# Gating a two-layer encoder's heads: where the product of heads and gates is made

## The chip, the cores and the metric

One core of one Trainium2 chip runs the whole program. Five engines work side by side and are tied together by semaphores only: TensorE (PE; its weight loads are shown apart as PEld), VectorE (DVE), ScalarE (ACT), GpSimd (POOL) and SyncE (SP), which here does nothing but issue transfers, in order. The metric is device microseconds per execution, the median of several runs. TensorE's clock has two levels, 2.4 and 1.2 GHz; the profile gives the granted share.

## What is computed

Two sequences (1024 and 512 tokens, width 1024) go through two layers and a final RMSNorm, all in float32. Layer 0 puts an attention of 8 heads (A) beside a retention of 4 heads (B); layer 1 is a windowed attention of 16 heads (C). In both, a gate of the same width as the heads is projected from the same input, goes through SiLU, and multiplies the heads before the one output projection:

```python
# layer 0
mixed = jnp.concatenate([jax.nn.silu(ga) * oa, jax.nn.silu(gb) * ob], axis=-1)
return x + mixed @ w_out
# layer 1
o = banded_sink_gqa(q, k, v, sink, rel_bias)
return x + (jax.nn.silu(gate) * o) @ w_out
# last
return rmsnorm(x, final_norm)
```

Only the place of the product `silu(gate) * o` is at stake here. Its values stay the same.

## The kernel before

**Tiling.** Tokens come in 12 blocks of 128, grouped into three groups t = 0, 1, 2 of 512 (0 and 1 are the long sequence, 2 the short one), and are worked on in the order 2, 0, 1. The width is split into 8 slices k of 128 rows, so that heads, gates and activations are 24 tiles [128, 512], one for each k and t. Every matmul runs on float32 operands split into a high and a low part (`X["h"]`, `X["l"]`, `split`), three products each. Layer 0's slices 0 and 1 hold the first four heads of A (g = 0), 2 and 3 the other four (g = 1), and 4 to 7 the heads of B. In layer 1, chunk c holds slices 2c and 2c+1.

**Attention.** `pipeline` (L722) goes through units of one head group and one 128-token block. For each unit `front_a` or `front_c` makes scores and softmax weights: VectorE takes maxima, ScalarE exponentiates, GpSimd scales the weights by the reciprocal sum (`scale_pool`, L107, tiles `e` and `ec`). `Back.T` transposes them, `Back.PV` multiplies by the values, and `Back.evac` (L700) brings the result `oT` [128, 2 x 128] from PSUM into SBUF. From there it is stored to DRAM (`o_ab` in layer 0, `o_c` in layer 1, L711). The buffers of tag O that hold `olo` and `oT` are two.

**Fillers.** While a unit passes through the other engines, TensorE gets filler steps of three matmuls: the gate projections (`gate_stream`, `gate_pieces`: 8 steps for each k and t, tile `psg`; then SiLU on VectorE, ScalarE and GpSimd, and a store of the finished gate to `g_ab` or `g_c`, L222), in layer 1 also the projections of the next queries (`psq`), and, once a group's attention is over, that group's output projection (`out_proj_fm`, tile `pso`).

**The mix.** When group t's attention is done, `hook_a` or `hook_c` calls `mix_fm` (L257): for each slice k it loads the heads and the gate back from DRAM into the two halves of one tile `mo`, multiplies them on GpSimd (L262) and splits the product into `X["h"]` (ScalarE, L117) and `X["l"]` (VectorE, L118) for the output projection. For some units the heads don't go to DRAM: `Back.mix` (L713) loads the unit's gates (`gq`, two transfers), multiplies on GpSimd (L719) and splits at once. That is so for g = 1 with t < 2 in layer 0 (8 units), and for c = 3 with t = 1 in layer 1 (4 units). Slices 2 and 3 of the last group never go through `mix_fm`.

**Order.** Each engine's queue is in order. A scheduler sets it from the order in which the code is written, from `tc.high_priority()` stretches and from its own view of the engines' times. A transfer that waits for its data or its buffer holds everything behind it on SP; likewise a product on GpSimd that waits for a gate holds the scalings behind it.

## Time and profile before

| | us |
|---|---|
| median of 3 runs | 1507.81 (1505.19 to 1508.24) |
| the profiled execution | 1507.83 |
| its span, first to last instruction | 1506.1 |
| TensorE busy | 1451.7 (96%) |
| VectorE busy | 1052.6 (70%) |
| GpSimd busy | 812.3 (54%) |
| ScalarE busy | 719.5 (48%) |

The program has stages: up to 300 us the input, keys and values and the retention; 310 to 590 us layer 0's attention with the gates as filler; 590 to 800 us the rest of that attention with the mix and the output projection; 800 to 920 us the last third of that projection and layer 1's keys; 920 to 1290 us layer 1's attention with gates and queries as filler; 1290 to 1460 us its end with the mix and the output projection; then the last third of the projection. A busy share over the whole span mixes these, so what counts is read by stage: which engines are nearly full there, where TensorE is idle, and which waits the chain goes through. Matmuls overlap, so a TensorE that reads as fully busy is not proven to be at its peak; the number of matmuls in a stretch (the x counts) says more.

### The profile page before, as it was taken

The page shows a single profiled execution, that of the slowest core. Times are in us where ns is not written, and L with a number is a line of the kernel's source. Part 1 is how long each engine was busy: PE and PEld are TensorE (multiplying, and loading weights), DVE is VectorE, ACT ScalarE, POOL GpSimd, SP SyncE. Part 2 cuts the span into 40 slices and gives each one's busy share as a digit, 9 for nine tenths or more (in the row PEclk, how much of TensorE's full clock was granted, in tenths as well). Part 3 has the DMA queues.
Part 4 walks back from the last instruction along what each step waited for, and adds up shares of the span by engine and source line. Part 5 has one row for each costly group of instructions (what it writes and reads, how often), then busy time and mean ns, then how long its engine had stood idle before and what let it go on. Part 6 is the DMA issues. An engine that isn't in the chain of part 4 may idle for free.

```text
span 1506.1 us, 26020 instructions
## 1 busy us (share of the span) xinstructions
PE 1451.7 (96%) x8734; PEld 1269.8 (84%) x8734; DVE 1052.6 (70%) x2431; ACT 719.5 (48%) x1770; POOL 812.3 (54%) x1044
## 2 busy tenths in 40 slices
PE   8999999989999999999999999999999999999997
PEld 8989999977888888777778998888888888777777
DVE  7455867686676666887978237687777767888774
ACT  5632222354555555555653245566556556645202
POOL 7654654474645484887887423342522532566542
PEclk9999999999999999999999999999999999999999
DMA  9631212326212143643664231121212211568752
GB/s 329 207 119 51 75 54 69 99 74 191 74 45 72 53 113 116 206 141 107 192 213 141 86 109 46 61 71 50 74 45 94 63 54 53 173 206 280 229 157 99
DMA packets 137333, 176.59 MB, mean 117 GB/s; under 512 B 38064, under 2 KB 66736, under 8 KB 137200
## 3 DMA queue, kind: packets, MB, share of 16 engines
q1 hardware_dynamic: 135040, 169.41, 35.8%
q0 software_dynamic: 2016, 5.51, 1.3%
q8 instruction: 69, 1.13, 0.3%
q14 instruction: 64, 0.52, 0.1%
q10 hardware_dynamic: 144, 0.01, 0.0%
HBM read 125.83 MB, written 53.25 MB: 119 GB/s over the span
## 4 chain that ended last, share of the span: by engine, by line
PE 71%; DVE 11%; DMA 4%; POOL 4%; issue 3%; ACT 1%; SPq 0%; POOLq 0%; DVEq 0%; ACTq 0%
PE psg L89 17%; PE psq L89 10%; PE po L89 8%; PE psb L89 8%; PE pso L89 8%; PE pte L173 7%; PE s L89 4%; PE sc L89 4%; PE pskv L89 2%; DVE xl L118 2%; DVE w L140 1%; DVE el L112 1%; DMA wraw<-in_woc 1%; DVE nm L837 1%; PE ptq L173 1%
## 5 line engine op out<-in xcount | busy, mean ns | idle before, releaser
L89 PE MATMUL psg<-xh,wg 128*128 128x512 f32 x768 | 263.9, 400 | 0.2 <-POOL wg L140 0.2
L107 POOL TENSOR_SCALAR ec<-ec,rl 128x384 f32<-128x384 f32 (+1 forms) x192 | 108.8, 581 | 241.5 <-DVE rl L1056 87.7
L112 DVE TENSOR_TENSOR el<-pte,eh 128x512 fp32r<-128x512 f32 x288 | 196.6, 685 | 56.2 <-ACT eh L111 32.5
L111 ACT ACTIVATE eh<-pte 128x512 fp32r<-128x512 f32 x288 | 170.1, 596 | 119.7 <-PE po L89 65.0
L89 PE MATMUL pso<-xh,w 128*128 128x512 f32 x512 | 183.6, 418 | 10.4 <-DVE w L140 4.6
L89 PEld LDWEIGHTS psg<-xh,wg 128*128 128x128 f32 x768 | 143.9, 189 | 29.2 <-POOL e L107 0.9
L107 POOL TENSOR_SCALAR e<-e,rl 128x512 f32<-128x512 f32 x160 | 114.3, 726 | 93.3 <-DVE rl L848 33.9
L89 PE MATMUL psg<-xl,wg 128*128 128x512 f32 x384 | 150.9, 393 | 0.0
L1051 ACT ACTIVATE ec<-ec,nm 128x384 f32<-128x384 f32 (+1 forms) x192 | 109.6, 572 | 82.7 <-DVE nm L1049 77.7
L845 ACT ACTIVATE e<-s,nm 128x512 f32<-128x512 f32 x160 | 108.9, 687 | 68.0 <-DVE nm L842 50.0
L837 DVE TENSOR_REDUCE nm<-s 128x1 f32<-128x512 f32 x160 | 107.8, 683 | 37.4 <-PE s L89 36.9
L139 POOL TENSOR_SCALAR w<-wraw 128x512 fp32r<-128x512 f32 x116 | 79.4, 686 | 97.6 <-PE pskv L89 32.4
L89 PE MATMUL psq<-xh,w 128*128 128x512 f32 x384 | 130.0, 397 | 0.0
L89 PEld LDWEIGHTS pso<-xh,w 128*128 128x128 f32 x512 | 99.4, 197 | 35.8 <-DVE w L140 7.8
L1045 DVE CUSTOM_DVE_ANT_0 ec<-sc,bias,sink_s 128x384 f32<-128x384 f32 (+1 forms) x192 | 105.3, 568 | 22.2 <-PE sc L89 17.8
L89 PE MATMUL pso<-xl,w 128*128 128x512 f32 x256 | 104.1, 408 | 2.0 <-DVE xl L118 2.0
L173 PE MATMUL pte<-ident,e 128*128 128x128 f32 x640 | 96.0, 275 | 1.6 <-POOL e L107 0.8
L173 PEld LDWEIGHTS pte<-ident,e 128*128 128x128 f32 x640 | 78.8, 142 | 20.3 <-ACT e L845 2.2
L140 POOL TENSOR_TENSOR w<-wraw,w 128x512 fp32r<-128x512 f32 x68 | 91.2, 1344 | 1.9
L89 PEld LDWEIGHTS psg<-xl,wg 128*128 128x128 f32 x384 | 72.5, 189 | 13.1
L89 PEld LDWEIGHTS psq<-xh,w 128*128 128x128 f32 x384 | 71.9, 188 | 13.6
L173 PE MATMUL pte<-ident,ec 128*128 128x128 f32 x512 | 79.0, 272 | 0.2
(230 smaller groups left out, 3942.6 us busy)
## 6 DMA issues: line engine op xcount, KB each, us to landing
wraw<-in_woab SPq DMA_DIRECT2D x48, 256.0 KB, 3.4
wraw<-in_woc SPq DMA_DIRECT2D x48, 256.0 KB, 3.8
wraw<-in_wab SPq DMA_DIRECT2D x44, 256.0 KB, 3.3
wraw<-in_wc SPq DMA_DIRECT2D x36, 256.0 KB, 3.1
xt<-in_xT SPq DMA_DIRECT2D x24, 256.0 KB, 5.4
xb<-in_x SPq DMA_DIRECT2D x24, 256.0 KB, 4.8
qd<-qd SPq DMA_DIRECT2D x48, 128.0 KB, 2.9
gab<-gz SPq DMA_DIRECT2D x24, 256.0 KB, 2.0
```

What stands on the lines that cost most here:

```text
L89: i = nc.tensor.matmul(ps, lhsT=lhsT, rhs=rhs, start=start, stop=stop)
L107: nc.gpsimd.tensor_scalar(o, i, s, 1.0, ALU.mult, ALU.mult)
L111: nc.scalar.activation(hi, src, AF.Copy)
L112: nc.vector.tensor_tensor(lo, src, hi.bitcast(F32), ALU.subtract)
L118: nc.vector.scalar_tensor_tensor(lo, src, scale, hi.bitcast(F32), ALU.mult, ALU.subtract)
L139: nc.gpsimd.tensor_scalar(w[:, 0, :], raw, 1.0, 1.0, ALU.mult, ALU.mult)
L140: (lo or nc.gpsimd).tensor_tensor(w[:, 1, :], raw, w[:, 0, :].bitcast(F32), ALU.subtract)
L173: return nc.tensor.transpose(o, i, ident)
L837: nc.vector.tensor_reduce(nm2[:, c:c + 1] if nh == 2 else nm[:, h:h + 1], s, AX.X, ALU.max, negate=True)
L845: nc.scalar.activation(eh[c], ss[c], AF.Exp, bias=nm[:, h:h + 1], accum_out=l[:, h, c:c + 1])
L1045: nc.vector.tensor_tensor_reduce(es[h][:, :nk], s, bias[h][:, bo:bo + nk], 1.0, sink_s[:, 4 * c + h:4 * c + h + 1], ALU.add, ALU.max, mx[: ...
L1051: nc.scalar.activation(es[a][:, :nk], es[a][:, :nk], AF.Exp, bias=nm[:, a:a + 1], accum_out=l[:, a:a + 1])
```

## The change

The product is made as soon as the later of heads and gate exists.

- **Layer 0, gates that come after their heads.** The gates of slices 4 to 7 are projected first, then 2 and 3, then 0 and 1. Where the heads of a gate are already stored, the finished gate is not stored: the heads are loaded (`go`, a buffer of tag `wraw`), and GpSimd multiplies the gate tile by them when the next piece has done its fourth step; only the product goes to `g_ab`. 18 of the 24 gates are of this kind (slices 0, 1, 4 to 7). `mix_fm` then loads one tile and multiplies nothing.
- **Layer 0, heads that come after their gates.** The 8 units of g = 1 and t < 2 load their gates when their second transpose is issued, and no longer at the evacuation, and the product is made as two products [128, 128] on VectorE instead of one [128, 256] on GpSimd. Slices 2 and 3 of t = 2 stay with two loads and a product in `mix_fm`.
- **Layer 1.** The gates are filled one set earlier (in the set before the first unit too), so that each unit finds its gates in DRAM. Every unit loads them early, two transfers of [128, 128], into unused columns of the bias tiles (which grow from 384 to 512 columns). 44 units multiply on GpSimd, two products [128, 128] between evacuation and store; the last 4 (c = 3, t = 1) multiply on VectorE. `mix_fm` loads one tile for each slice.

```diff
@@ -199,10 +199,20 @@
             hs.append(h)
         return hs
 
-    def gate_pieces(w, j, k, t, gd, scale):
+    stored, gated, owed = {}, set(), []
+
+    def settle():
+        while owed:
+            owed.pop(0)()
+
+    def gate_pieces(w, j, k, t, gd, od, scale):
+
+
         ps = ps_p("psg")
         for kk in range(KT):
             proj_fm_k(ps, w, j * P, t, kk)
+            if kk == 3:
+                settle()
             if kk < KT - 1:
                 yield
         with tc.high_priority():
@@ -219,15 +229,27 @@
             else:
                 nc.gpsimd.tensor_scalar(th, th, 1.0, 1.0, ALU.add, ALU.mult)
                 nc.gpsimd.tensor_tensor(z, th, z, ALU.mult)
+        if stored.get((id(od), k, t)) == GB:
+            o = wp.tile([P, 2 * CW], F32, tag="wraw", name="go", bufs=2)
+            dma(out=o, in_=od[k][t])
+            gated.add((id(gd), k, t))
+
+            def product():
+                nc.gpsimd.tensor_tensor(z, z, o, ALU.mult)
+                dma(out=gd[k][t], in_=z)
+            owed.append(product)
+        else:
             dma(out=gd[k][t], in_=z)
         yield
 
-    def gate_stream(warr, c0, gd, scale=None):
-        for c in range(4):
+    def gate_stream(warr, c0, gd, od, chunks, scale=None):
+        for c in chunks:
+            settle()
             w = load_w(warr, c0 + c, "wg")
             for t in ORDER:
                 for j in range(2):
-                    yield from gate_pieces(w, j, 2 * c + j, t, gd, scale)
+                    yield from gate_pieces(w, j, 2 * c + j, t, gd, od, scale)
+        settle()
 
     class Fill:
         def __init__(self, gen, rate):
@@ -257,9 +279,12 @@
     def mix_fm(t, ks, od, gd):
         for k in ks:
             o, g = stage("mo")
-            dma(out=o, in_=od[k][t])
-            dma(out=g, in_=gd[k][t])
-            nc.gpsimd.tensor_tensor(o, o, g, ALU.mult)
+            if gd is None or (id(gd), k, t) in gated:
+                dma(out=o, in_=(od if gd is None else gd)[k][t])
+            else:
+                dma(out=o, in_=od[k][t])
+                dma(out=g, in_=gd[k][t])
+                nc.gpsimd.tensor_tensor(o, o, g, ALU.mult)
             split_x(o, k, t, 0.5)
             yield
 
@@ -645,6 +670,7 @@
             oT = buf("H", "oT")
             nc.scalar.activation(oT, pt, AF.Copy)
             dma(out=o_ab[4 + h][(b0 + i0) // GB], in_=oT)
+            stored[id(o_ab), 4 + h, (b0 + i0) // GB] = GB
 
     def bias_table():
         oh = buf("H", "oh")
@@ -678,6 +704,8 @@
             self.po = None
 
         def T(self, kb):
+            if kb == 1 and self.gd is not None:
+                self.load_gates()
             pt = ps_t("pte")
             for h in range(4):
                 i = transpose(pt[:, h * P:(h + 1) * P], self.eget(h, kb))
@@ -707,16 +735,31 @@
                 nc.vector.tensor_tensor(oT[64 * c:64 * c + 64], pov[:, :, c, :], lov[:, :, c, :], ALU.add)
             if self.gd is not None:
                 return self.mix(oT)
+            self.store(oT)
+
+        def store(self, oT):
             for a in range(2):
                 dma(out=self.od[self.k0 + a][self.t][:, self.j * P:(self.j + 1) * P], in_=oT[:, a, :])
+                key = id(self.od), self.k0 + a, self.t
+                stored[key] = stored.get(key, 0) + 1
+
+        def load_gates(self):
+            if self.od is o_ab:
+                g = buf("Q", "gq", 256)
+                self.g = [g[:, :P], g[:, P:]]
+            else:
+                self.g = [bias_c[self.k0 // 2][2 * (self.j % 2) + a][:, 384:512] for a in range(2)]
+            for a in range(2):
+                dma(out=self.g[a], in_=self.gd[self.k0 + a][self.t][:, self.j * P:(self.j + 1) * P])
 
         def mix(self, oT):
-            g = buf("Q", "gq", 256) if self.od is o_ab else stage("gq")[0][:, :256]
-            g = g.rearrange("p (a q) -> p a q", a=2)
             sl = slice(self.j * P, (self.j + 1) * P)
+            if self.od is o_c and (self.k0, self.t) != (6, 1):
+                for a in range(2):
+                    nc.gpsimd.tensor_tensor(oT[:, a], oT[:, a], self.g[a], ALU.mult)
+                return self.store(oT)
             for a in range(2):
-                dma(out=g[:, a, :], in_=self.gd[self.k0 + a][self.t][:, sl])
-            nc.gpsimd.tensor_tensor(oT, oT, g, ALU.mult)
+                nc.vector.tensor_tensor(oT[:, a], oT[:, a], self.g[a], ALU.mult)
             for a in range(2):
                 k = self.k0 + a
                 if self.j == 0:
@@ -804,7 +847,7 @@
         yield from q_pieces_a(1, load_w(wab, 6, "w"), rq1, True)
         rbuild()
         bias_table()
-        yield from gate_stream(wab, 7, g_ab, lambda t: group(R, t))
+        yield from gate_stream(wab, 7, g_ab, o_ab, (2, 3, 1, 0), lambda t: group(R, t))
 
     kv_a = {}
 
@@ -957,7 +1000,7 @@
 
     class FillC:
         def __init__(self):
-            self.gates, self.cur, self.acc, self.more = gate_stream(wc, 5, g_c), iter(()), 0.0, []
+            self.gates, self.cur, self.acc, self.more = gate_stream(wc, 5, g_c, o_c, range(4)), iter(()), 0.0, []
 
         def fill_set(self, n):
             if n < 4 * NG:
@@ -968,10 +1011,9 @@
             for j in range(2):
                 if n < 4 * NG:
                     yield from q_pieces(self.w, j, t, qs[n])
-                if n > 0:
-                    for _ in range(9):
-                        if next(self.gates, self) is not self:
-                            yield
+                for _ in range(9):
+                    if next(self.gates, self) is not self:
+                        yield
 
         def start(self, n):
             for _ in self.cur:
@@ -1004,9 +1046,9 @@
 
     def load_bias(c):
         if c not in bias_c:
-            bias_c[c] = [buf("E", "bias", 384) for h in range(4)]
+            bias_c[c] = [buf("E", "bias") for h in range(4)]
             for h in range(4):
-                dma(out=bias_c[c][h], in_=bass.AP(btab_d.tensor, btab_d.offset + (4 * c + h) * P * 512 + 127,
+                dma(out=bias_c[c][h][:, :384], in_=bass.AP(btab_d.tensor, btab_d.offset + (4 * c + h) * P * 512 + 127,
                                                   [[511, P], [1, 384]]))
 
     def load_c(c, names, out):
@@ -1059,7 +1101,7 @@
             if h < 3:
                 yield 0
         return Back(lambda h, kb: es[h][:, kb * P:(kb + 1) * P], k1 - k0, lambda kb: vget_c(c, k0 + kb), o_c, 2 * c, t, j,
-                    g_c if (c, t) == (3, 1) else None)
+                    g_c)
 
 
     def fin_out(t, k, y, rb):
@@ -1077,8 +1119,8 @@
             if t == 2:
                 late.clear()
             drain(ahead)
-            drain([mix_fm(t, KS_C if t else KS_C[6:], o_c, g_c)])
-            ahead.append(mix_fm(0 if t else 1, KS_C[:6], o_c, g_c))
+            drain([mix_fm(t, KS_C if t else KS_C[6:], o_c, None)])
+            ahead.append(mix_fm(0 if t else 1, KS_C[:6], o_c, None))
             fillc.more.append(out_proj_fm(t, woc, KS_C, lambda k: x1T_d[k][t], x2T_d, fin_out, None if t else late, nc.vector, t == 0))
 
     pipeline([(c, b) for c in range(4) for b in BLOCKS], prep_c, front_c, BUFS["E"] - 4,
```

What the scheduler makes of it at three places. Layer 0, GpSimd, from the last gates of the filler to group 2's mix (`e` are softmax weights, `w` output weights being split, `gz` and `th` gates, `acc` sums of squares). Before:

```order
L221 TENSOR_TENSOR gz_7569<-th_7571,gz_7569 128x512
L107 TENSOR_SCALAR e_7452<-e_7452,rl_7257 128x512
L107 TENSOR_SCALAR e_7453<-e_7453,rl_7257 128x512
L262 TENSOR_TENSOR mo_7675<-mo_7675 128x512
L262 TENSOR_TENSOR mo_7683<-mo_7683 128x512
L262 TENSOR_TENSOR mo_7691<-mo_7691 128x512
L107 TENSOR_SCALAR e_7470<-e_7470,rl_7257 128x512
L107 TENSOR_SCALAR e_7471<-e_7471,rl_7257 128x512
L262 TENSOR_TENSOR mo_7699<-mo_7699 128x512
L220 TENSOR_SCALAR th_7670<-th_7670 128x512
L262 TENSOR_TENSOR mo_7707<-mo_7707 128x512
```

Now:

```order
L238 TENSOR_TENSOR gz_7719<-gz_7719,go_7725 128x512
L140 TENSOR_TENSOR w_7806<-wraw_7804,w_7806 128x512
L107 TENSOR_SCALAR e_7646<-e_7646,rl_7562 128x512
L107 TENSOR_SCALAR e_7647<-e_7647,rl_7562 128x512
L139 TENSOR_SCALAR w_7811<-wraw_7809 128x512
L107 TENSOR_SCALAR e_7664<-e_7664,rl_7562 128x512
L107 TENSOR_SCALAR e_7665<-e_7665,rl_7562 128x512
L140 TENSOR_TENSOR w_7811<-wraw_7809,w_7811 128x512
L139 TENSOR_SCALAR w_8085<-wraw_8083 128x512
L287 TENSOR_TENSOR mo_7765<-mo_7765 128x512
L140 TENSOR_TENSOR w_8085<-wraw_8083,w_8085 128x512
L287 TENSOR_TENSOR mo_7773<-mo_7773 128x512
```

Before, group 2's products (eight in all) stand in a burst between the softmax scalings; now the last of the 18 early products (L238) stands before them, and of the burst two products are left, behind the output weights.

Layer 1, SP, where group 2's heads and gates are fetched for the mix (`oc` heads, `gc` gates, the number is the tile's). Before:

```order
L711 DMA oc_143<-oT 128x128
L711 DMA oc_146<-oT 128x128
L222 DMA gc_166<-th 128x512
L260 DMA mo<-oc_125 128x512
L261 DMA mo<-gc_149 128x512
L260 DMA mo<-oc_128 128x512
L261 DMA mo<-gc_152 128x512
L260 DMA mo<-oc_131 128x512
L261 DMA mo<-gc_155 128x512
```

Now:

```order
L283 DMA mo<-oc_125 128x512
L283 DMA mo<-oc_128 128x512
L283 DMA mo<-oc_131 128x512
L283 DMA mo<-oc_134 128x512
L742 DMA oc_136<-oT 128x128
L742 DMA oc_139<-oT 128x128
L283 DMA mo<-oc_137 128x512
L283 DMA mo<-oc_140 128x512
L242 DMA gc_169<-th 128x512
```

Each pair of loads has become one, and six of the eight loads for this group stand ahead of all stores of its last chunk (`oc_143`, `oc_146`), where before they stood behind the first of these.

Layer 1, GpSimd, some units in the middle of the attention (`ec` softmax weights, `oT` evacuated heads, `bias` the columns that hold the gate). Before:

```order
L107 TENSOR_SCALAR ec_12366<-ec_12366,rl_12304 128x384
L107 TENSOR_SCALAR ec_12367<-ec_12367,rl_12304 128x384
L107 TENSOR_SCALAR ec_12487<-ec_12487,rl_12447 128x256
L107 TENSOR_SCALAR ec_12488<-ec_12488,rl_12447 128x256
L107 TENSOR_SCALAR ec_12489<-ec_12489,rl_12447 128x256
L107 TENSOR_SCALAR ec_12490<-ec_12490,rl_12447 128x256
```

Now:

```order
L107 TENSOR_SCALAR ec_12512<-ec_12512,rl_12444 128x384
L759 TENSOR_TENSOR oT_12589<-oT_12589,bias_11307 128x128
L759 TENSOR_TENSOR oT_12589<-oT_12589,bias_11308 128x128
L107 TENSOR_SCALAR ec_12619<-ec_12619,rl_12571 128x256
L107 TENSOR_SCALAR ec_12620<-ec_12620,rl_12571 128x256
L759 TENSOR_TENSOR oT_12702<-oT_12702,bias_11309 128x128
L759 TENSOR_TENSOR oT_12702<-oT_12702,bias_11310 128x128
L107 TENSOR_SCALAR ec_12621<-ec_12621,rl_12571 128x256
L107 TENSOR_SCALAR ec_12622<-ec_12622,rl_12571 128x256
```

Where only scalings stood, each unit's two products now stand between them.

## Rows read from the trace of the kernel before

**Rows 1.** The page: an engine's busy time; a costly DVE group (busy, mean ns).

```profile
PE 1451.7 (96%) x8734; PEld 1269.8 (84%) x8734; DVE 1052.6 (70%) x2431; ACT 719.5 (48%) x1770; POOL 812.3 (54%) x1044
...
L112 DVE TENSOR_TENSOR el<-pte,eh 128x512 fp32r<-128x512 f32 x288 | 196.6, 685 | 56.2 <-ACT eh L111 32.5
```

**Rows 2.** Stretches: length, busy PE, PEld, DVE, ACT, POOL; clock, DMA share, GB/s.

```profile
360.00:590.00 230.00, 230.00 (x1180) 190.65 (x1179) 149.68 (x315) 121.22 (x272) 124.41 (x155) 1.00 0.29 86
590.00:660.00 70.00, 64.30 (x312) 50.89 (x311) 57.52 (x102) 40.60 (x89) 57.98 (x58) 0.98 0.63 199
...
720.00:800.00 80.00, 76.50 (x394) 61.05 (x392) 65.45 (x112) 44.12 (x96) 68.17 (x69) 0.98 0.64 200
920.00:1290.00 370.00, 369.68 (x1920) 313.46 (x1919) 271.78 (x859) 216.30 (x590) 132.72 (x210) 1.00 0.20 59
1290.00:1350.00 60.00, 55.73 (x254) 45.05 (x253) 51.69 (x121) 31.60 (x79) 39.62 (x43) 0.91 0.67 214
1350.00:1410.00 60.00, 55.00 (x263) 43.32 (x262) 51.16 (x114) 29.60 (x73) 41.40 (x46) 0.98 0.85 276
```

**Rows 3.** The chain that ended last, 590 to 665 us: start, us, what.

```profile
592.81 3.00 DMA mo<-gab
...
595.97 1.29 POOL mo L262
...
617.66 5.12 DMA mo<-gab
...
644.46 0.75 POOL oT L719
```

**Rows 4.** Groups of DVE, then POOL, 590 to 800 us (busy us, mean ns | idle).

```profile
L118 DVE SCALAR_TENSOR_TENSOR xl<-mo,xh 128x512 fp32r<-128x512 f32 x20 | 20.4, 1018 | 5.0 <-ACT xh L117 4.9
L842 DVE TENSOR_TENSOR nm<-nm 128x1 f32<-128x1 f32 x30 | 16.6, 552 | 0.2
L847 DVE TENSOR_TENSOR rl<-l 128x1 f32<-128x1 f32 x30 | 11.8, 395 | 8.8 <-ACT e L845 8.7
...
L848 DVE RECIPROCAL rl<-rl 128x1 f32<-128x1 f32 x30 | 4.8, 160 | 0.7
...
L262 POOL TENSOR_TENSOR mo<-mo 128x512 f32<-128x512 f32 x20 | 26.5, 1331 | 5.8 <-DMA mo<-gab 5.5
...
L719 POOL TENSOR_TENSOR oT<-oT,gq 128x256 f32<-128x256 f32 x7 | 5.6, 804 | 0.0
```

**Rows 5.** The same chain, 1290 to 1410 us.

```profile
1300.24 2.69 DMA mo<-oc
...
1333.17 5.15 DMA mo<-gc
...
1338.48 1.30 POOL mo L262
...
1387.07 5.96 DMA y<-x1T
```

**Rows 6.** Groups of DVE, then POOL, 1290 to 1410 us.

```profile
L118 DVE SCALAR_TENSOR_TENSOR xl<-mo,xh 128x512 fp32r<-128x512 f32 x21 | 19.8, 945 | 2.8 <-ACT xh L117 2.7
L140 DVE TENSOR_TENSOR w<-wraw,w 128x512 fp32r<-128x512 f32 x22 | 19.6, 896 | 4.4 <-POOL w L139 4.3
...
L1055 DVE TENSOR_TENSOR l<-l,se 128x2 f32<-128x2 f32 x15 | 6.9, 461 | 3.0 <-ACT se L1054 3.0
...
L262 POOL TENSOR_TENSOR mo<-mo 128x512 f32<-128x512 f32 x22 | 30.2, 1372 | 15.7 <-DMA mo<-gc 11.5 <-DMA mo<-oc 3.1 <-PE psg L89 1.1
```

**Rows 7.** Tile oT: xcount: ns min/median/max, first to last start.

```profile
L711 SPq DMA_DIRECT2D oc<-oT x88: 319/423/888, 924.6 to 1362.0; - x88
...
L118 DVE SCALAR_TENSOR_TENSOR xl<-oT,xh x24: 275/367/1376, 645.6 to 1405.7; 128x128 fp32r<-128x128 f32 x24
...
DMA to landing us min/median/max: 1.5/1.6/6.5
```

**Rows 8.** Waits of POOL over the span: us in total, times, longest us.

```profile
POOL ec L107 <- DVE rl L1056: 87.7, 33, 9.9
```

## The prediction

> **What bounds the kernel now.** First comes the page's engine line: TensorE is busy for 1451.7 of 1506.1 us, so a gain can hardly come from other engines' sums, only from the stretches where TensorE stands still [rows 1]. The table by stretches shows where these are. From 360 to 590 and from 920 to 1290 us, where the filler runs, it is busy throughout (230.00 of 230, 369.68 of 370), while DVE is at 65 and 73% and POOL at 54 and 36% [rows 2]. It stands still in the two stages in which heads and gates are mixed: 5.70 us in 590 to 660, 3.50 us in 720 to 800, 4.27 and 5.00 us in the two stretches from 1290 to 1410; in these four DVE is at 82 to 86% and the DMA engines at 63 to 85% [rows 2]. The matmul counts say the same more strongly: 4.23 per us from 1290 to 1350 against 5.19 from 920 to 1290. The granted clock, a mean of the two levels 1.2 and 2.4 GHz, is below 1.00 only in the stretches with pauses, 0.91 from 1290 to 1350.
>
> The chain says what TensorE lacks in these stages. Between 590 and 660 us it goes through two loads for the mix (3.00 and 5.12 us), through products of the mix on POOL (one of 1.29 us is shown, in others it comes in pieces), and through a late unit's product on POOL (0.75 us) [rows 3]. Between 1290 and 1410 us it goes through loads of 2.69 and 5.15 us and a product of 1.30 us [rows 5]. These are the operations that the change moves.
>
> A second thing shows in the groups. DVE operations with two inputs in SBUF are long where POOL is busy: a [128, 1] minimum takes 552 ns and a [128, 1] sum 395, against 160 ns for the reciprocal of the same size with one input; `xl<-mo,xh` takes 1018 ns where `el<-pte,eh`, with one input in PSUM, takes 685 [rows 1, 4]. So POOL's work is in part DVE's waiting time. The Trainium skill says why ("SBUF — State Buffer", Who interferes with whom): a VectorE instruction with two SBUF inputs and a GpSimd instruction that reads SBUF exclude each other, and the second to start waits for the whole of the first. These rows agree with it.
>
> **The change part by part.** The sum is made on the profiled execution, 1507.83 us with its span of 1506.1; the median of the runs is 1507.81, so nothing is to be converted.
>
> *Layer 0, 590 to 660 us.* Group 2's mix has 16 loads and 8 products; 10 loads and 2 products are left (slices 2 and 3 keep both). If the chain's two loads shrink with the number of loads, 8.12 x 6/16 = 3.0 us go; of a shown product of 1.29 us three quarters, 1.0 us; the late unit's 0.75 us goes whole, since its gates are loaded long before and the product is in DVE's own queue. That is 4.8 us, and the pause in TensorE of 5.70 us lets no more than that be gained. Against it: what is late next is DVE, already at 82%. I take 3.
>
> *Layer 0, 720 to 800 us.* The same for the other groups, but the pause is only 3.50 us and much of that stretch belongs to the end of the projection, which stays. I take 1.
>
> *DVE and POOL in these 210 us.* POOL loses 18 products of 1.331 us and 8 of 0.804, 30.4 us in all [rows 4]. DVE gets 16 products [128, 128] with two SBUF inputs. Their nearest row is `xl<-oT,xh`, of the same size and also with two inputs: 275 ns at least, 367 as the median, 1376 at most [rows 7]. At the median that is 16 x 0.367 = 5.9 us; the ends are 4.4 and 22. DVE gets back part of its waiting: over the three groups (1018 - 685) x 20 = 6.7, (552 - 160) x 30 = 11.8 and (395 - 160) x 30 = 7.1 us, 25.6 us together. POOL is busy for 126.2 of the 150 us in the two stretches shown, 84%, so for 177 of the 210 us at most; 30.4 of them are 17%, so at least 4.4 us of the waiting go; more if two-input operations on POOL do most of the blocking. The two cancel out: 0, with no term in the sum.
>
> *Layer 1, 1290 to 1410 us.* Each pair of loads becomes one, and six of group 2's eight stand before the stores of its last chunk. Of the chain's 2.69 + 5.15 = 7.84 us between a half and three quarters go, 3.9 to 5.9, and the product's 1.30. POOL loses 22 products of 1.372 us, 30.2 us of its 81.0 here [rows 6], and gets some 10 short ones. A third of that comes off DVE's waiting: (945 - 685) x 21 = 5.5, (896 - 685) x 22 = 4.6 and (461 - 160) x 15 = 4.5 us, so 14.6 x 0.33 = 4.9 us, from which 8 new products take 8 x 0.367 = 2.9. That makes 3.9 + 1.3 + 2.0 = 7.2 to 9.2 us; the pauses, 9.27 us, are the bound. The load of a residual that follows in the chain, 5.96 us [rows 5], doesn't get shorter by as much. I take 7.
>
> *The early products, 360 to 610 us.* 18 products of 1.29 to 1.33 us and 18 loads. POOL goes from 54% to about 64%, TensorE is full, so they cost nothing while the filler lasts. The cover gone, the last two pieces' products would lie before group 2's mix: 2.7 us.
>
> *Layer 1's products, 924 to 1362 us.* 88 products [128, 128]. Their price isn't in the trace: not under half of 804 ns (half the size), not over 804 [rows 4]; from 256 to 512 columns the time grows by 1331 - 804 = 527 ns, so half of that less than 804, 0.54 us, is my value. 88 x 0.54 = 48 us on a POOL at 36% in 920 to 1290 us. Per unit it is 1.1 us, with units (437.4 / 44 =) 9.9 us apart [rows 7]. What waits behind it: the next scalings on POOL, the store, and on SP what stands behind that store and behind the two gate loads. Under a full TensorE: 0 us.
>
> *Moved gates.* 18 filler steps go from layer 1's end to its beginning. The matmuls are the same and TensorE is full at both places: 0. They leave the mix at 1290 us with less cover, which is why I stay below the bound there.
>
> Sum: -3 - 1 - 7 = -11, so 1507.8 - 11 = 1497, rounded.
>
> **The rivals.**
>
> *Slower: layer 1's heads hold their buffer.* `oT` shares two buffers with `olo`. Till now it was free after a store of 1.6 us; now it has to wait for POOL to reach the products, for the products and for the store. POOL's scalings wait 87.7 / 33 = 2.7 us at a time for DVE's reciprocals, and up to 9.9 [rows 8], and the product stands behind them. 2.7 + 1.1 + 0.4 + 1.6 = 5.8 us, under the 9.9 between units, so on the mean it fits. It decides from a wait of 7 us on: then the next unit's evacuation stands in DVE's queue, and with it the maxima and reciprocals behind it. If a third of 44 units lost 1 us each and TensorE ran dry for it, +15; with the gain, 1512. For it: in-order queues on three engines. Against it: TensorE has no pause in 370 us now, and DVE and POOL are a quarter idle or more.
>
> *No change: the pauses have another cause behind them.* In both stages DVE is at 82 to 86%, and other loads stand in the chain (5.96 us). If DVE only fills up with what waited, 8 of the 11 us come back: 1505. For it: the chain goes through DVE in long stretches between the loads. Against it: DVE itself waits for POOL.
>
> *The direct products cost a whole lock.* If each of the 24 new DVE products had to let a POOL operation pass first, as the longest row has it (1376 ns), they would cost 24 x 1.0 = 24 us more than at the median, in the two stages where DVE is fullest; half of it on the path would be +12, so 1509. The median of 367 speaks against it. The skill's rule on the shared port, cited above, would allow it: it says that the order of issue decides who waits.
>
> *More than forecast.* All pauses of the four stretches end: 5.70 + 3.50 + 9.27 = 18.5 us, and with the lower clock's share 1487 to 1489.
>
> **How the numbers follow.** The forecast, with everything from 1490 to 1504, has 0.60; more than that 0.08; no change 0.14; the slower mechanism 0.13; the lock 0.05. A measurement of this kernel tells about 0.2% (3 us) from no change. Faster by over that: the first two, 0.68. Within it: no change and a part of the lock, 0.17. Slower: 0.15. The range goes from all pauses gone (1487) to the lock's 1509; it leaves out the upper part of the slow case and the lowest of the best, together under 2 in 10.
>
> **What would show it.** Right: TensorE's idle time in the two mixing stages falls by half or more; the loads for the mix are gone from the chain around 1300 to 1340 us; `xl<-mo` and the [128, 1] operations get shorter in both stages; layer 1's attention keeps a full TensorE, with products near 0.5 us. Wrong: pauses of TensorE between 920 and 1290 us whose release is DVE's evacuation or a store; SP waiting for POOL's `oT` longer than a unit; the direct products on DVE near 1 us; or the old pauses at 600 and 1330 us still there, released by `w` and `y` in place of `mo`.

## The result: slower by 2.8%

The changed kernel takes 1549.53 us (1543.78 to 1554.24) where the kernel before took 1507.41 on the same chip: a ratio of 1.0276, interval 1.0251 to 1.0301. The forecast was 1497, its range ended at 1509. The profiled execution took 1543.78 us, its span is 1542.0, 35.9 us more than before.

The page's engine line, and the table by stretches of after (us, PE, PEld, DVE, ACT, POOL busy, granted clock, DMA share, GB/s), to be read against [rows 1] and [rows 2]:

```profile
PE 1464.7 (95%) x8734; PEld 1275.2 (83%) x8734; DVE 1054.8 (68%) x2455; ACT 717.2 (47%) x1770; POOL 809.1 (52%) x1098
```

```profile
590.00:660.00 70.00, 60.75 (x282) 47.29 (x281) 54.72 (x97) 37.44 (x82) 47.85 (x50) 0.95 0.56 166
720.00:800.00 80.00, 71.04 (x356) 56.81 (x356) 67.90 (x120) 43.71 (x97) 61.23 (x62) 0.98 0.51 157
920.00:1290.00 370.00, 365.75 (x1867) 307.56 (x1867) 262.56 (x798) 202.23 (x551) 156.32 (x267) 1.00 0.24 72
1290.00:1350.00 60.00, 53.14 (x256) 42.67 (x254) 46.31 (x151) 35.06 (x97) 19.92 (x37) 0.94 0.26 79
1350.00:1410.00 60.00, 57.73 (x279) 45.68 (x280) 51.67 (x135) 35.80 (x89) 34.57 (x50) 1.00 0.71 221
1410.00:1470.00 60.00, 53.76 (x227) 42.86 (x226) 33.61 (x72) 14.72 (x35) 21.41 (x26) 0.91 0.66 206
```

TensorE stands still for 9.25 us in 590 to 660 (5.70 before) and for 8.96 in 720 to 800 (3.50 before); in layer 1's attention for 4.25 (0.32 before). Over the whole span the engines do nearly the same work as before (GpSimd 809.1 us after 812.3, VectorE 1054.8 after 1052.6, the same 8734 matmuls). The products did leave the mix: layer 1's end lies 43 us later now, and in its 120 us from 1333 to 1453 GpSimd is busy for 56.91 us, where it was for 81.01 from 1290 to 1410; the DMA engines are at 65% after 76%. TensorE's pauses there are 9.76 us after 9.27: emptier engines, and no shorter pause. So the loss is in order and in cover, not in work.

Three stretches show where. **Layer 0's second stage.** The chain that ended last, after, 590 to 612 us (start, us, what):

```profile
591.89 2.76 PE psg L89 x12
...
595.04 4.38 DMA wraw<-in_woab
...
599.50 1.10 POOL w L139
...
600.67 1.30 POOL w L140
...
601.99 3.99 DMA wraw<-in_woab
```

Where group 2's mix stood [rows 3], the chain now waits for the raw output weights and their splitting. These had been prefetched. The tile `wraw` from 520 to 640 us, before and then after (duration ns min/median/max, first to last start):

```profile
L135 SPq DMA_DIRECT2D wraw<-in_woab x10: 328/333/422, 536.5 to 632.7; - x10
```

```profile
L135 SPq DMA_DIRECT2D wraw<-in_woab x10: 328/351/838, 595.0 to 640.0; - x10
```

The first load is issued 58.5 us later. `go`, the heads loaded for the early product, has the tag of the raw weights and takes turns in their two buffers; each of these buffers now holds a `go` until the next gate piece's fourth step, and the output weights queue up behind the last gates.

**Layer 1's start.** The chain after, 893 to 918 us, and then before in the same stretch:

```profile
893.19 6.00 PE pskv L89 x50
...
899.89 1.26 POOL w L140
...
901.16 3.16 DMA wraw<-in_wc
...
905.17 1.29 POOL w L140
906.48 5.00 DMA wraw<-in_wc
...
911.56 0.63 POOL wg L139
...
912.23 2.08 PE psg L89 x4
```

```profile
893.95 13.61 PE psq L89 x60
907.57 0.96 PE sc L89 x8
908.52 5.45 PE psg L89 x24
```

The first set now wants gate weights too. They go through the same two raw buffers as the query weights, which are split only when the keys' projection is through.

**Layer 1's end.** The matmuls of gates (`psg`) and output projection (`pso`) from 1240 us on, before, then after:

```profile
L89 PE MATMUL psg<-xh,wg x55: 387/389/485, 1240.0 to 1299.0; 128*128 128x512 f32 x55
L89 PE MATMUL pso<-xh,w x151: 387/393/765, 1307.7 to 1399.7; 128*128 128x512 f32 x151
```

```profile
L89 PE MATMUL psg<-xh,wg x49: 387/392/487, 1239.9 to 1295.2; 128*128 128x512 f32 x49
L89 PE MATMUL pso<-xh,w x97: 388/389/506, 1337.3 to 1400.0; 128*128 128x512 f32 x97
```

Before, group 2's last heads are evacuated at 1306.3 us, and the projection that needs them begins at 1307.7; the last gate products lie in front of it. After, the projection begins at 1337.3 with what is there, and these heads come at 1349.0, 43 us later than before; the gates end at 1295, and there is little with which TensorE could bridge. Of the 43 us, 25.6 are there already at layer 1's first evacuation (949.3 us after 923.7), in part because a set of gate products now runs ahead of it; at the end of the program 35.9 are left. The chain of after goes through the heads' store and the loads of the mix one by one:

```profile
1350.44 3.49 DMA oc<-oT
1354.00 2.62 DMA mo<-oc
...
1359.98 4.57 DMA mo<-oc
...
1394.40 3.84 DMA mo<-oc
1400.62 4.94 DMA mo<-oc
```

No product stands between these any more, so ScalarE's split waits for the loads itself (14 times, 17.8 us from 1300 to 1500) where it had waited for GpSimd (12 times, 26.9 us). The halved mix is visible; it is overrun by what was lost ahead of it.

### The profile page after: what moved, and what is told of

It reads as the page before. It is cut to its first block, busy times and chain, and to the rows that moved or that the text cites. A ratio compares the mean times of both kernels' runs of the same rounds, so it can differ in the third digit from the quotient of the medians.

```text
span 1542.0 us, 26266 instructions
## 1 busy us (share of the span) xinstructions
PE 1464.7 (95%) x8734; PEld 1275.2 (83%) x8734; DVE 1054.8 (68%) x2455; ACT 717.2 (47%) x1770; POOL 809.1 (52%) x1098
## 4 chain that ended last, share of the span: by engine, by line
PE 65%; DVE 10%; DMA 9%; issue 4%; POOL 4%; ACT 3%; SPq 1%; POOLq 0%; DVEq 0%; ACTq 0%
PE psg L89 15%; PE psq L89 10%; PE psb L89 8%; PE pso L89 7%; PE po L89 7%; PE pte L173 6%; PE s L89 3%; PE sc L89 3%; DMA mo<-oc 2%; PE pskv L89 2%; DMA wraw<-in_woc 2%; DVE xl L118 1%; ACT e L888 1%; DVE el L112 1%; DMA wraw<-in_woab 1%
## 5 line engine op out<-in xcount | busy, mean ns | idle before, releaser
L759 POOL TENSOR_TENSOR oT<-oT,bias 128x128 f32<-128x128 f32 x88 | 40.2, 478 | 97.5 <-DVE oT L735 51.5
```

The costliest lines, as they stand in the source:

```text
L759: nc.gpsimd.tensor_tensor(oT[:, a], oT[:, a], self.g[a], ALU.mult)
```

## The experiments

All ratios are to the kernel before on the same chip. The times of different rows come from several chips, so prices below are differences of ratios, in us of some 1509, where nothing else is said.

| kernel | us | ratio (95%) |
|---|---|---|
| the change | 1549.53 | 1.0276 (1.0251 to 1.0301) |
| layer0_only | 1522.77 | 1.0074 (1.0050 to 1.0097) |
| layer1_only | 1530.63 | 1.0122 (1.0092 to 1.0151) |
| gates_one_set_early | 1521.71 | 1.0077 (1.0049 to 1.0105) |
| mix_light | 1499.65 | 0.9922 (0.9901 to 0.9943) |
| l0_own_heads_buffer | 1514.05 | 1.0017 (1.0004 to 1.0030) |
| l0_direct_only | 1513.50 | 1.0015 (1.0002 to 1.0028) |
| early_gates_early_weights | 1517.30 | 1.0041 (1.0026 to 1.0055) |
| l1_products_on_vector | 1533.03 | 1.0140 (1.0123 to 1.0156) |
| gates_eight_steps | 1515.69 | 1.0043 (1.0029 to 1.0056) |
| l1_no_gate_no_product | 1521.24 | 1.0075 (1.0053 to 1.0096) |
| l1_product_no_load | 1526.75 | 1.0117 (1.0093 to 1.0141) |
| change_mended | 1510.68 | 1.0012 (0.9996 to 1.0028) |
| mended_nine_steps | 1525.85 | 1.0108 (1.0093 to 1.0123) |
| mended_late_weights | 1514.28 | 1.0027 (1.0014 to 1.0039) |
| mended_shared_buffers | 1523.15 | 1.0082 (1.0067 to 1.0097) |
| layer1_mended | 1509.55 | 1.0005 (0.9990 to 1.0021) |
| layer1_mended_even | 1510.15 | 1.0004 (0.9992 to 1.0016) |
| change_mended_even | 1511.00 | 1.0013 (1.0000 to 1.0025) |

### The halves of the change, and two of its parts alone

layer0_only is the change with layer 1 as before; layer1_only is the reverse, by these lines (no early products, early gate loads in layer 1 alone, layer 0's gates in the old order) and by the old product on GpSimd in layer 0's 8 units:

```diff
-        if stored.get((id(od), k, t)) == GB:
+        if False:
...
-            if kb == 1 and self.gd is not None:
+            if kb == 1 and self.gd is g_c:
...
-        yield from gate_stream(wab, 7, g_ab, o_ab, (2, 3, 1, 0), lambda t: group(R, t))
+        yield from gate_stream(wab, 7, g_ab, o_ab, range(4), lambda t: group(R, t))
```

> The change in layer 0 alone (early products at the gates, gates of slices 4 to 7 first, direct products on VectorE), layer 1 as in the kernel before. Theory A, the loss is the sum of separate stalls, each in its stage: by TensorE's idle time the changed kernel loses some 11 us between 590 and 870 us, so this one is 11 us over before, 1518, and TensorE stalls at 606, 650 and 700 to 775 us as there. Theory B, the kernel before is tuned to one order and any disturbance of the order costs, layer 1 above all: then nothing in particular is tied to layer 0, and the time lies nearer 1530, with stalls also behind 900 us. The prediction's own terms for layer 0 (-3 and -1) would give 1503.

> The change in layer 1 alone, layer 0 as in the kernel before. Theory A: idle of TensorE lost at the start of layer 1 (6 to 7 us), in its attention (8 us) and in its end (13 us) makes 27 us, so 1535. Theory B: about 1530 too, but with the stalls at other places than in the changed kernel. The prediction's term for layer 1 (-7) would give 1500.

Both halves lose, 0.7% and 1.2%; together they lose 2.8%, more than the sum of 2.0%. The kernel before with layer 1's early gates alone, and with a light mix alone (in `mix_fm` of both layers):

```diff
-                if n > 0:
-                    for _ in range(9):
...
+                for _ in range(9):
...
```

```diff
             dma(out=o, in_=od[k][t])
-            dma(out=g, in_=gd[k][t])
-            nc.gpsimd.tensor_tensor(o, o, g, ALU.mult)
```

> The kernel before with one edit: layer 1's gates are filled from the first set on. Theory A: the first gate weights are now wanted at 908 us together with the first query weights, and two buffers for raw weights bring them too late; TensorE waits 6 to 7 us for GpSimd's split at the start of layer 1, and nothing else changes: 1514. Prediction: the moved matmuls cost nothing, 1507.

> The kernel before, where the mix in both layers loads the heads alone and leaves out the load of the gate and the product, so 42 loads and 42 GpSimd products are missing (the gate is left out of the result). If the mix's loads and products held TensorE up, as the prediction has it, this alone gives -11 us or more: 1497. If ScalarE, which splits the tile next, now takes the wait for the load that GpSimd took before, the gain is small or nothing: 1504 to 1510, with ScalarE waiting for the mix's loads some 30 us in all.

mix_light is what the prediction hoped to gain, and it is there: 0.78%, 11.8 us of 1508. Its trace, of the slowest of its four runs, puts the gain where the sum put most of it. Layer 1's first head is evacuated 4.4 us later than before (928.1 against 923.7) and the end comes 5.5 us earlier, so 9.9 us are gained behind that point. That layer 0 gains nothing isn't shown by this: layer 1's keys' projection begins at 854.8 us here and at 850.4 before, but in the traces of the nine other kernels that leave layer 0 as it was it begins anywhere from 847.3 to 855.5. The early gates, which the prediction had at zero, cost 0.77%, as much as the mix brings.

### Layer 0: whose buffer it is

l0_own_heads_buffer is layer0_only with one line changed; l0_direct_only has the direct products and nothing else of the change:

```diff
-            o = wp.tile([P, 2 * CW], F32, tag="wraw", name="go", bufs=2)
+            o = buf("Q", "go")
```

> layer0_only with one edit: the heads that the early product loads (go) take a buffer of tag Q, no longer one of the two buffers for raw weights. Theory A1: in layer0_only the go tiles hold those two buffers until the last gate, so the output projection's first six weight loads come at 595 us and later instead of at 536 to 555 us, and TensorE waits for them and for all that follows at 606 us and later; freed, these loads come early again, the 12 us are gone and some of the lighter mix's gain shows: 1505 to 1511. Rival A2: the direct products on VectorE (275 to 1379 ns each) in the fullest stretch of VectorE cost it: then it stays at 1519 to 1523.

> Layer 0's direct products on VectorE with early gate loads alone: no early products at the gates, gates in the order of before, the mix with both loads and GpSimd's product, layer 1 as before. A1: 1509 to 1512, as before, with the output weights loaded from 536 us. A2: most of layer0_only's loss, 1518 to 1523.

One tag takes layer 0's loss from 0.74 to 0.17%. The raw weights in l0_own_heads_buffer, the same row as above, are back in their old place:

```profile
L135 SPq DMA_DIRECT2D wraw<-in_woab x10: 327/333/424, 537.6 to 631.2; - x10
```

The direct products alone cost 0.15% (1.0002 to 1.0028), hardly clear of nothing and as much as is left.

### Layer 1: weights, engine, loads, hold

early_gates_early_weights is gates_one_set_early with its first weights loaded ahead of the keys' projection; l1_products_on_vector is layer1_only with its 88 products on VectorE. The edit of the first, then that of the second:

```diff
     wkv = load_w(wc, 0, "w")
+    wg0 = [load_w(wc, 5, "wg")]
...
-            w = load_w(warr, c0 + c, "wg")
+            w = wg0.pop() if warr is wc and c == 0 else load_w(warr, c0 + c, "wg")
```

```diff
-                    nc.gpsimd.tensor_tensor(oT[:, a], oT[:, a], self.g[a], ALU.mult)
+                    nc.vector.tensor_tensor(oT[:, a], oT[:, a], self.g[a], ALU.mult)
```

> gates_one_set_early with one edit: layer 1's first gate weights are loaded and split ahead of the key projection, where GpSimd is idle. If the 9 us of idle TensorE between 875 and 950 us are a wait for those weights, they go and the time falls from 1521.7 to 1513; what is left over the kernel before (2 to 5 us) is then the lost cover at layer 1's end. If the early gates hurt by something else (the attention starts later and the chain after it is latency bound), it stays at 1519 or more.

> layer1_only with one edit: the 88 products between evacuation and store are made on VectorE, right behind the evacuation, no longer on GpSimd. If the heads' buffer is held too long by GpSimd's queue (the slower rival of the prediction), the 6 to 8 us of stalls between 925 and 1300 us go and some of the end's too: 1520 to 1524. If the products' engine doesn't matter, 1528 to 1533; if VectorE is short of time, more.

Early weights take the price of the early gates from 0.77 to 0.41% (the intervals overlap a little; the wait itself is plainly gone). The waits of TensorE's weight loads from 880 to 925 us hold three rows in gates_one_set_early, of which the first is

```profile
PEld psg L89 <- POOL wg L139: 3.4, 1, 3.4
```

and none in early_gates_early_weights. The engine of the products makes no difference, so the queue of GpSimd isn't what layer 1 loses by. The next three ask what is: fewer gate steps in a piece, so that 16 of 192 are left for the end (a set then has 32 filler steps and not 34, and the filler's rate is lowered with it); layer1_only without loads and products; and the same with the products, but on columns of the bias tiles that lie there anyway.

```diff
-RATE_C, RATE_T = 3.40, 3.40
+RATE_C, RATE_T = 3.20, 3.40
...
-                for _ in range(9):
+                for _ in range(8):
```

```diff
-            if kb == 1 and self.gd is g_c:
+            if kb == 1 and self.gd is g_c and (self.k0, self.t) == (6, 1):
                 self.load_gates()
...
-                    nc.gpsimd.tensor_tensor(oT[:, a], oT[:, a], self.g[a], ALU.mult)
+                    nc.gpsimd.tensor_tensor(oT[:, a], oT[:, a], bias_c[self.k0 // 2][2 * (self.j % 2) + a][:, 128:256], ALU.mult)
```

> The kernel before with the gates of the change (one set of heads early) and their first weights loaded ahead of the keys' projection, as in early_gates_early_weights (1517.3 us, ratio 1.0041), and now 8 gate steps in each piece of layer 1's attention instead of 9, so that 16 of the 192 steps (48 products) are left for the end of layer 1's attention. Theory (lost cover): the rest of what the early gates cost, about 6 us, is that no gate products are left on TensorE while the last heads are evacuated; then this run is near 1511 to 1512. Rival (the early products themselves crowd the attention that they are put into): the run stays at 1517. The prediction on record, in which moved gates cost nothing, would say 1507 to 1511 for all three.

> Layer 1's part of the change alone (layer1_only: 1530.6 us), with neither the loads of the gate tiles nor the products in the 44 evacuations of layer 1 that take them; the gate is left out of most of layer 1, so this is a kernel with less work. What stays is the early gate products on TensorE (+11 us in gates_one_set_early) and the light mix (-11 us in mix_light). Theory (loads and products at the evacuation are the second loss in layer 1): about 1512. Rival (what costs is that the output projection starts too early for the heads, whatever the evacuation does): stays within 5 us of 1530. The prediction, which put the loads and the products at nothing, has this run equal to layer1_only.

> As l1_no_gate_no_product, with the 88 products kept at the evacuation, but on columns of the bias that lie in SBUF all the time, in place of gate tiles loaded from memory; the gate itself is left out. It divides the price of the second loss in layer 1. If it is the products (the heads' buffer is held from the evacuation to the store, and the store comes later): near layer1_only, 1530. If it is the loads (44 more transfers of 128 KB on the queue in front of the mix's own): near l1_no_gate_no_product, 1512. The prediction says that neither costs anything.

gates_eight_steps gains nothing over early_gates_early_weights: with the old, slow mix, cover at the end isn't what is missing. For the other two the table says: the products cost 0.42% (1.0117 less 1.0075), 6.3 us, or 5.5 by the medians, which are of one chip here (1526.75 - 1521.24). The loads cost 0.05% more (1.0122 less 1.0117), 0.8 us: nothing that these runs can tell from zero. The products' price isn't tied to GpSimd, since VectorE makes them no cheaper. TensorE in 930 to 1300 us, in l1_no_gate_no_product and in l1_product_no_load (columns as above):

```profile
930.00:1300.00 370.00, 367.85 (x1901) 310.92 (x1899) 270.58 (x851) 215.88 (x583) 129.16 (x205) 1.00 0.22 64
```

```profile
930.00:1300.00 370.00, 364.26 (x1862) 305.41 (x1861) 268.25 (x818) 207.90 (x564) 155.90 (x268) 1.00 0.22 64
```

The pauses lie where one chunk of heads gives way to the next, and SP's waits of 925 to 1300 us name what differs there. For its bias loads SP waits in l1_product_no_load and in the change (us in total, times, longest us):

```profile
SPq L1056 <- PE pte L173: 15.2, 3, 5.4
```

```profile
SPq L1051 <- PE pte L173: 12.1, 3, 4.6
```

In l1_no_gate_no_product and in the kernel before, these loads wait only for DVE (longest 2.2 and 0.4 us). Bias tiles and softmax weights share the twelve buffers of tag E, of which the pipeline may fill eight and the bias four. A bias tile whose columns the product reads is held until the chunk's last head is out; the new one has to take a buffer that a transpose sets free, and fewer are left for scores. All eleven kernels here whose products read bias columns in layer 1 have these waits for transposes, and none of the others has.

Two other causes look less likely. The stores of the heads make SP wait no longer than before (161.4 us, at most 10.9 at a time, in l1_product_no_load; 156.3 and 11.8 before), and no evacuation there waits for a store between 925 and 1300 us. A late bias alone need not cost either: in gates_eight_steps, without such products, the bias loads wait for DVE for 10.5 us in three times, and TensorE is all but full:

```profile
930.00:1300.00 370.00, 368.61 (x1921) 312.18 (x1920) 279.12 (x886) 221.53 (x608) 136.50 (x218) 1.00 0.20 60
```

That the hold is the price is argued from these waits and from the place of the pauses, not shown: buffers of their own for these gates were not tried. So how the price divides between the late bias and the missing score buffers stays open too.

### The three causes taken away together, and put back one by one

change_mended is the whole change with `go` in tag Q, the first gate weights early, and eight steps; three kernels each undo one of these (mended_nine_steps undoes the filler's rate with the steps); layer1_mended has its layer 1 and the layer 0 of before.

> The whole change (1549.5 us) with three causes taken away: layer 0's gate tile in another tag than the raw weights' (12 us of layer 0's loss, by layer0_only and l0_own_heads_buffer: 9 regained), the first gate weights of layer 1 loaded ahead of the keys' projection (4.4 us regained in early_gates_early_weights), and 8 gate steps in a piece instead of 9 (0 to 6 us). Theory (the causes are separate and add): 1549.5 - 9 - 4.4 - 5 = about 1531, with 1525 to 1537. Rival (the end of layer 1 is bound by the last evacuations and swallows what is gained ahead of it): 1540 or more. The prediction's 1497 would need all of them gone.

> change_mended (1510.7 us, where the sum of the parts said 1531) with 9 gate steps in a piece again, so that no gate products are left for the end of layer 1's attention; the other two mends stay. Theory C (cover: with the light mix the output projection begins beside the last heads, and then gate products kept for that place count, although they made no difference in gates_eight_steps, where the mix was still the slow one): 1522 to 1530. Theory W (weights: it is the first weights that were late, and eight steps are worth nothing): 1509 to 1514.

> change_mended with the first gate weights of layer 1 loaded where the change loads them, behind the keys' projection; layer 0's gate tile stays out of the raw weights' buffers and the 8 steps stay. By theory C of mended_nine_steps it costs the 4.4 us that it cost the gates alone: 1515. By theory W it carries nearly all of what the parts' sum missed: 1530 or more.

> change_mended with layer 0's gate tile back in the two buffers of the raw weights. If layer 0's loss stands by itself, as layer0_only and l0_own_heads_buffer say, it costs 8.7 us: 1519 to 1520. If what layer 0 loses is partly regained behind it (there are 80 us of pure projection between), it is less: 1512 to 1515.

> Layer 1's part of the change alone, with its first gate weights early and 8 steps; layer 0 stays as before. This is layer1_only (1530.6 us) with two mends. If layer 0's part, even mended, costs what l0_own_heads_buffer says (3 us), this run is 1507 to 1508, no different from before; if the light mix brings here what it brought in mix_light (11 us) and the early gates cost only the 2 to 3 us that are left of them, it is 1501 to 1504, faster than both kernels. The rival (loads and products at the evacuation cost in layer 1 what l1_no_gate_no_product took off, 9 us) gives 1515.

Three edits of a line or two take back 2.64 of the 2.76%. Put back one at a time, nine steps cost 0.96% (14.5 us), the shared buffers 0.70% (10.6 us), the late weights 0.15% (2.3 us, with intervals that overlap). Theory C holds: the two matmul rows of above, in mended_nine_steps and then in change_mended, differ by what stands before the projection.

```profile
L89 PE MATMUL psg<-xh,wg x48: 387/392/487, 1241.7 to 1287.2; 128*128 128x512 f32 x48
...
L89 PE MATMUL pso<-xh,w x110: 387/392/628, 1329.0 to 1399.9; 128*128 128x512 f32 x110
```

```profile
L89 PE MATMUL psg<-xh,wg x77: 389/389/468, 1240.0 to 1318.3; 128*128 128x512 f32 x77
...
L89 PE MATMUL pso<-xh,w x136: 387/389/505, 1322.0 to 1399.4; 128*128 128x512 f32 x136
```

Gates up to 1318 fill the time until group 2's last heads are out, and by 1400 the projection has 136 of these products done instead of 110. In change_mended no load for the mix is left in the chain from 1300 to 1500 us. So the eight steps, with their rate, are worth nothing in gates_eight_steps, beside the old mix, and 14.5 us in change_mended, beside the light one. That it is the faster mix that gives cover this value is the likely reading; the two kernels differ in the other parts of the change as well.

The three single prices add to 1.81%, not to 2.64. The other 0.83%, some 12 us, are lost only when at least two of the causes stand together; which two was not tried, and stays open.

### What takes the rest

mix_light gains 0.78%, yet layer1_mended stands at 1.0005. Its trace has the pauses at the changes of chunk again, and there its filler runs out one place before the end of a set. Two kernels spread the steps evenly:

```diff
-            self.rate = RATE_C if n < 11 else RATE_T
+            self.rate = RATE_T if n > 10 else 3.22 if ORDER[(n - 1) % NG] == 2 else 2.93
```

> layer1_mended (1509.6 us, profiled span 1504.0) with its filler spread over the whole of each set of four blocks: a set has 32 filler steps and 10 or 11 places for them, and 3.22 or 2.93 steps a place end with the set, where 3.20 ran out one place early. In layer1_mended TensorE has nothing to do at the sets' ends (4.7 us of excess pitch in 1050 to 1075, about 13 us over 925 to 1300, where the kernel before has 4). If that is the price that is left of the early gates: 8 us less than layer1_mended, 1500 to 1503, faster than both kernels. If the gaps only move to other places (the rows of the softmax chain ec, eh, el are what is late, not the filler): 1507 to 1510, no different.

> change_mended (1510.7 us, ratio 1.0012) with the same even spread of layer 1's filler. The theory of layer1_mended_even gives 1502 to 1505; its rival 1508 to 1511. The difference to layer1_mended_even is what layer 0's part, mended, still costs: l0_own_heads_buffer says 3 us, the prediction says a gain of 4.

The rival holds: nothing changes, 1.0004 and 1.0013. The filler isn't what is short. In layer1_mended_even, SP's waits for the bias loads, and the stretches around the three changes of chunk, then the whole of the attention:

```profile
SPq L1057 <- PE pte L173: 18.1, 3, 7.0
```

```profile
1050.00:1075.00 25.00, 23.62 (x125) 19.17 (x124) 20.23 (x72) 16.17 (x49) 9.31 (x19) 1.00 0.17 50
...
1155.00:1180.00 25.00, 23.96 (x126) 19.84 (x125) 17.36 (x66) 16.02 (x52) 10.64 (x21) 1.00 0.19 58
...
1270.00:1295.00 25.00, 23.97 (x127) 19.90 (x127) 18.30 (x68) 15.38 (x49) 10.03 (x20) 1.00 0.09 27
```

```profile
930.00:1300.00 370.00, 364.81 (x1876) 304.87 (x1875) 276.57 (x861) 216.84 (x593) 164.84 (x286) 1.00 0.25 71
```

In the attention TensorE lacks 4.9 us against before, 3.45 of them in these 75 us, and 44 matmuls (x1876 against x1920; at 370 / 1920 = 0.19 us apiece 8.5 us). In mix_light, which has neither early gates nor a hold, it has x1915 and 369.68 us. So part of what takes back the gain of the light mix is, by these rows, what the products at the evacuation cost (0.42% above). The early gates are the rival: in gates_eight_steps, with early weights and eight steps and no such products, they still cost 0.43%, although TensorE is all but full in the attention. Each price is near half of the gain, but prices don't add here, and no kernel has the light mix and the mended early gates without the products. How the 0.78% divides stays open. Of all versions run, mix_light alone beats the kernel before, and it computes less; no complete kernel did.

## Why the prediction was wrong

The sum failed at the terms that it set to zero because TensorE is full where they run. Three of them stand first; the terms for the mix follow.

- **"The early products ... cost nothing while the filler lasts"** failed, for a reason that the section never weighed. POOL's time was right (18 products of 1292 ns, 23.3 us, under a full TensorE). The price is in the tile of the 18 loads: it takes the buffers through which weights come. l0_own_heads_buffer and mended_shared_buffers put it at 9 to 11 us. The diff showed the tag in plain sight.
- **Moved gates at 0** failed twice. At the new place the weights weren't there (1.0077 less 1.0041 is 5.4 us beside the old mix; 2.3 us in the mended change). At the old place the sum saw "less cover", and priced it at two or three us of caution; it is 14.5 us in the mended change (nine steps against eight, with the rate). "The matmuls are the same and TensorE is full at both places" says nothing of the operands at the new place, nor of what the old one had them for.
- **Layer 1's products at 0**: the size was right, 463 ns as the median for 0.54 us, 40.2 us in all for 48. The effect wasn't: the products cost 0.42%, 5.5 to 6.3 us, of the 1.2% of layer1_only, and the loads with them next to nothing. By which mechanism is argued (the hold of the bias tiles), not shown.
- **Layer 1, -7,** was right in mechanism, and too small by itself: in its trace mix_light gains 9.9 us behind layer 0. In the change it was overrun.
- **Layer 0, -3 and -1,** don't show. In mix_light's trace TensorE's pause in 590 to 660 does fall from 5.70 to 3.50 us, near the forecast, but in 720 to 800 it grows from 3.50 to 7.44. So it seems given back within the layer; a sure size would need more than one trace, as said above.
- **"The two cancel out"** for DVE and POOL was off in the change: a direct product in layer 0 takes 696 ns as the median, not 367, and `xl<-mo,xh` in 590 to 800 us stays at 980 ns (1018 before [rows 4]). But that came with the late weights: the same 16 products take 377 ns in l0_direct_only, near the estimate, and 290 in l0_own_heads_buffer, where `xl<-mo,xh` falls to 889. In layer 1's end the product takes 284:

```profile
L759 POOL TENSOR_TENSOR oT<-oT,bias x88: 448/463/917, 950.2 to 1391.8; 128x128 f32<-128x128 f32 x88
...
L762 DVE TENSOR_TENSOR oT<-oT,gq x16: 275/696/1379, 647.9 to 822.4; 128x128 f32<-128x128 f32 x16
...
L762 DVE TENSOR_TENSOR oT<-oT,bias x8: 277/284/291, 1408.0 to 1447.8; 128x128 f32<-128x128 f32 x8
```

- **The slower rival** had the sign and a wrong place. Heads do wait longer in their buffer, but the next evacuation waited for a store once, for 2.3 us, and l1_products_on_vector, which takes GpSimd's queue out of it, is no faster. If a held tile costs TensorE time there, it is the bias, not the heads. The rival of the lock was right in the rows of layer 0 (up to 1379 ns) and small in the sum: l0_direct_only, with all 16 of layer 0's products, costs 0.15%.
- Of the signs named, the last one came: "the old pauses at 600 ... still there, released by `w`". Two others came in form only: TensorE pauses in layer 1's attention, but only 0.4 us of that waits for an evacuation; and SP waits for POOL's `oT` for up to 10.9 us, longer than a unit, but before it waited up to 11.8 for DVE's. The chance of 0.15 for slower had only mechanisms of single operations in it; buffers and prefetches were no case.

## To carry to other kernels

For every tile that a change adds, ask whose buffers it takes and what was prefetched through them; a tile that is read later than before (here the bias) is held longer, and its successor has to find another buffer. For filler that is moved, price both places: are its operands there at the new one, and what bridges the wait at the old one. A part that is worth nothing alone can be worth 14 us beside another part, so a sum of single prices needs the parts tried together.

## What was not expected of the hardware

A VectorE product [128, 128] with both inputs in SBUF took 284 ns as the median in layer 1's end, where POOL is busy for 36% of the time (21.41 of 60 us), and 696 in layer 0's second stage, where it is busy for 68 to 77%; after `go` had another tag, the same 16 products took 290 with GpSimd busy for 67 to 74% in the same stretches (l0_own_heads_buffer). The Trainium skill ("SBUF — State Buffer", Who interferes with whom) lets the second of two such instructions wait for the whole of the first; the maxima of 1379 to 1383 ns agree, since 1383 - 284 = 1099 ns is less than one product [128, 512] on GpSimd (1292 ns for L238). That one changed tag moves the median by a factor of 2.4, with GpSimd about as busy, was not foreseen, and what in the order does it stays open.
